# An FFN up projection by seven block products: 15 of 22 channel pairs a layer, weight sums made by accumulating transfers, W_down in four parts

## The chip, the cores and the metric

The kernel runs on one core of a Trainium2 chip in one launch. The metric is the device time in microseconds. A core has TensorE (PE, the matmuls; PEld is its loading of weights), VectorE (DVE), ScalarE (ACT), GpSimd (POOL) and SyncE (SP, which here only issues DMA). Each runs its own instructions in order and waits on semaphores for the others.

## The reference

Two layers of a decoder trunk over 512 tokens with 16 meta tokens ahead of them (L = 528), width 1024, all in float32. Each layer has a mixer (eight heads of attention with a forget gate, a convolution module, a short gated convolution, one input and one output projection) and an FFN. What matters here is the FFN:

```python
def ffn_sublayer(h, pre_g, post_g, w_up, conv_w, w_down):
    u = rms_norm(h, pre_g)
    z = jnp.einsum("bld,df->blf", u, w_up)          # 1024 -> 2 x 2816
    z = causal_depthwise_conv(z, conv_w)            # 3 taps along the tokens
    g, up = jnp.split(z, 2, axis=-1)
    y = jnp.einsum("blf,fd->bld", jax.nn.silu(g) * up, w_down)
    return h + rms_norm(y, post_g)
```

## The kernel before

Activations lie with channels on the 128 partitions and tokens along the free axis. A float32 product is made from three float32r products: every operand is split into hi (a rounded copy, by ACT) and lo (the rest, by DVE), and `mm3` issues hi by hi, lo(u) by hi(w) and hi(u) by lo(w). Half of the tokens, 264, is one matmul's width. In layer 1 the meta tokens are not needed at the end, so the halves are 250 (two tokens ahead for the taps) and 264, and in W_down one matmul of 512 takes the place of two halves in all parts but the last.

W_up has 44 tiles of 128 output channels, in 22 pairs: pair f is gate tile f and up tile 22 + f. A tile is 8 blocks of input channels x 3 x 2 halves = 48 matmuls into a pair of PSUM banks (`mmt` takes the pairs by turns). u is kept without its token factor rz; `scaled` multiplies the sums by rz while moving them from PSUM to one of four tiles z0 to z3. `ffn_gate` then makes the taps (`gate_conv`: the first tap on ACT, two on DVE), Silu on ACT, the product on DVE, and the split of the result into yhi and ylo. A group of pairs is a part (`PARTS`, 8, 7 and 7 pairs); after the pairs of a part, W_down is multiplied with them for all eight output tiles m, and the sums are copied (part 0) or added (later parts) into yp. The last part's W_down is mixed with the final norm by a planner (`finish`).

Weights stream from memory. `prep_one` loads one tile of W (512 KB, raw, three buffers, on SP's queue), and ACT and DVE split it into whi and wlo (three buffers each); `next_w` keeps two tiles ahead. Outside the planner's sections, which are `manual_schedule`, the framework's scheduler puts the instructions of each engine in order from the dependences in the code; pools of tiles with a count of buffers decide which instruction waits for which.

Of the kernel before, what the change touches and what calls it, by code (L numbers as in the profile page):

```python
# [9 lines left out]
F32 = mybir.dt.float32  # L10
# [14 lines left out]
CK = 31  # L25
DFF = 2816
NF = DFF // P
PARTS = (8, 7, 7)
AHEAD = 2
CHUNK = 1056  # L30

# [309 lines left out]
def tile_hybrid_trunk(ctx: ExitStack, tc: tile.TileContext, xT, wflat, pv_d, out):  # L341
# [89 lines left out]
    def half_sl(hf):  # L431
        return slice(H * hf, H * (hf + 1))

    def load_h(pool, src, prio=0, also=()):


        t = T(pool, [P, KD, L], F32, "h", 1)
        at = {}
        for hf in range(2):
            for k0 in range(0, KD, 2):  # L440
                eng, queue = ("act", nc.scalar) if (hf, k0) in also else ("sp", nc.sync)
                after = [at[0, KD - 2]] if also and hf else []
# [6 lines left out]
    h_dram = T(dram, [P, KD, L], F32, "h_dram")  # L449
    g_dram = [T(dram, [2, HEADS, L], F32, f"g_dram{l}") for l in range(DEPTH)]  # L450


# [23 lines left out]
    def prep_one():  # L476
        i = wpos[0]
        if i >= len(chunks):
            return
        wpos[0] += 1  # L480
# [5 lines left out]
        nc.scalar.copy(hi[:, :sz], raw[:, :sz])  # L486
        nc.vector.tensor_sub(lo[:, :sz], raw[:, :sz], hi[:, :sz].bitcast(F32))  # L487
        ready.append((i, tuple(t[:, :sz].rearrange("p (k n) -> p k n", n=n) for t in (hi, lo))))

    def prefetch(n):  # L490

        while wpos[0] < len(chunks):
            if wpos[0] not in wide and sum(i not in wide for i, _ in ready) >= n:
# [157 lines left out]
    def two(t):  # L651
        return t.rearrange("p (a b) -> p a b", a=2)
# [920 lines left out]
    def finish(norms, h, h_at, spans, ks, rhs, y_at, yp, gpost, gpre, nsplit, first=None, rz=None, scaled=None,  # L1573
# [76 lines left out]

        def ends(hf):
            a, z = spans[hf]
            yield from post_norm(norms, ("y", hf), None if first is None else ("h", hf), h, [] if merge else list(h_at.values()), a, z, yp,
                                 gpost if merge and not GA else None, None if merge else gpre, first and first.at, hf, hf, out_at, y_out)
# [70 lines left out]
    for l in range(DEPTH):  # L1725
# [20 lines left out]
        with tc.tile_pool(name=f"fp{l}", bufs=2, reuse_waits="tile") as fp:  # L1746
# [35 lines left out]
            with tc.manual_schedule(engines=every):  # L1782
# [7 lines left out]
                       gains("mix_post_g"), gains("ffn_pre_g"), SPLIT["w_out"], first, rz, scaled_half, early)  # L1790
                plan_ends()

            def wtap(i, t):
                c = _COLS["ffn_w"] + 3 * t + i
                return pv[:, c:c + 1]

            def gate_conv(t, src, dst):

                nc.scalar.activation(dst, src[:, 2:2 + 2 * fw], AF.Copy, scale=wtap(2, t))  # L1799
                for i in (1, 0):  # L1800
                    nc.vector.scalar_tensor_tensor(dst, in0=src[:, i:i + 2 * fw], scalar=wtap(i, t), in1=dst,  # L1801
                                                   op0=ALU.mult, op1=ALU.add)

            def ffn_gate(f):

                cs = []
                for e, t in enumerate((f, NF + f)):
                    c = T(fp, [P, 2, H], F32, "c", 4).rearrange("p a b -> p (a b)")[:, :2 * fw]
                    gate_conv(t, zs[(2 * f + e) % len(zs)], c)
                    cs.append(c)  # L1810
                silu = nc.scalar.activation(cs[0], cs[0], AF.Silu)  # L1811
                if f == NF - 1:
                    with tc.issue_after(silu.ins):
                        nc.scalar.preload_act_table_set(EXPSET)
                nc.vector.tensor_mul(cs[0], cs[0], cs[1])  # L1815
# [3 lines left out]
                nc.scalar.copy(ghi, cs[0])  # L1819
                nc.vector.tensor_sub(glo, cs[0], ghi.bitcast(F32))  # L1820
                return ghi, glo

            g = {}
            f0 = 0
            for part, nf in enumerate(PARTS):
                for f in range(f0, f0 + nf):
                    for i in (2 * f, 2 * f + 1):
                        if i < len(zs):
                            continue
                        if i < FIRST["w_out"]:  # L1830
                            scaled(i, [first.ps[hf, i] for hf in range(2)])
                            continue
                        w = next_w()
                        ps = mmt()
                        mm3({hf: ps[:, hf, :iws[hf]] for hf in range(2)}, w, range(KD), u_in)
                        scaled(i, [ps[:, :, :H]] if i0 == 0 else [ps[:, hf, :iws[hf]] for hf in range(2)])
                    g[f] = ffn_gate(f)
                ks = list(range(nf))
                grhs = lambda b, k, hf, f0=f0: g[f0 + k][b][:, fw * hf:fw * (hf + 1)]
                if part < len(PARTS) - 1:  # L1840
                    for m in range(KD):
                        w = next_w()
                        ps = mmt()
                        if final:

                            mm3({0: ps[:, 0, :2 * fw]}, w, ks, lambda b, k, hf, f0=f0: g[f0 + k][b][:, :2 * fw])
                            d, src = yp[:, m, t0:], ps[:, 0, :2 * fw]
                        else:
                            mm3({hf: ps[:, hf, :fw] for hf in range(2)}, w, ks, grhs)
                            d, src = two(yp[:, m, t0:]), ps[:, :, :fw]  # L1850
                        if part == 0:
                            nc.scalar.copy(d, src)  # L1852
                        else:
                            nc.vector.tensor_add(d, d, src)  # L1854
                else:
                    gpre = None if final else pvs[l + 1][1][:, _COLS["mix_pre_g"]:]
                    first = None if final else First(u_rhs, [H, H], {})
                    with tc.manual_schedule(engines=every):
# [7 lines left out]
                        finish(norms, h, {}, o_spans, ks, grhs, lambda k, nf=nf: t_last if k == nf - 1 else [], yp,  # L1866
                               gains("ffn_post_g"), gpre, SPLIT["ffn_w_down"], first)
                f0 += nf
        if final:
# [50 lines left out]
```

## Time and profile before

| | |
|---|---|
| median of 3 runs | 1326.64 us (1325.96 to 1328.13) |
| profiled execution, first to last instruction | 1324.9 us, granted TensorE clock 0.990 |
| TensorE busy | 1280.9 us, 97%, 9798 instructions |
| VectorE busy | 878.9 us, 66% |
| ScalarE busy | 643.5 us, 49% |
| GpSimd busy | 107.7 us, 8% |
| DMA moved | 118.27 MB, mean 89 GB/s |

The profiled execution has no time of its own beside its span; the span is 1.7 us under the median of the runs. A row of a view by groups gives line, engine, operation, output and inputs, shape and count, then the busy time in us and the mean of one in ns, then the idle time of the engine just ahead of them and what ended it. A row of a timeline gives start, duration, the operation, and in brackets the idle time before it and what released it. L12 is line 12 of the kernel. Most of layer 0's FFN lies between 265 and 645 us.

### The profile page before, as it was taken

The numbers are of one execution on the slowest core, as the hardware profiler recorded it, in microseconds if no ns is written. First come the engines' busy times: TensorE is split into PE (matmuls) and PEld (weight loads), VectorE is DVE, ScalarE is ACT, GpSimd is POOL, SyncE is SP. The second block draws the span as 40 slices with busy tenths as digits, with TensorE's granted clock in tenths as the row PEclk, the third lists the DMA queues.
The fourth block names the chain that finished last, engine by engine and source line by source line (L and its number), as shares of the span: only waits on it lengthen the run. The fifth ranks groups of instructions, "written<-read, shape, count | busy, mean of one in ns | idle before, by whom it ended". The sixth has DMA issues, their size and how long they took to land. (4 is left out here: it accounts for less than half of the span.)

```text
span 1324.9 us, 24035 instructions
## 1 busy us (share of the span) xinstructions
PE 1280.9 (97%) x9798; PEld 1229.1 (93%) x9798; DVE 878.9 (66%) x1516; ACT 643.5 (49%) x1221; POOL 107.7 (8%) x267
## 2 busy tenths in 40 slices
PE   6999999999999999999989999999999999999996
PEld 6988988999999999999988989889999799989995
DVE  5698887588633664566675888866877247636765
ACT  7346668655423432334661566685643233313442
POOL 1313320000000000000003233200000000000000
PEclk8999999999999999999999999999999999999998
DMA  6132120612232222323240322216032233232321
GB/s 217 49 97 60 52 93 33 209 33 87 90 96 87 89 86 90 97 93 99 95 147 17 99 76 71 57 49 221 21 96 90 86 96 94 70 113 91 90 71 64
DMA packets 42702, 118.27 MB, mean 89 GB/s; under 512 B 4848, under 2 KB 15088, under 8 KB 42592
## 3 DMA queue, kind: packets, MB, share of 16 engines
q1 hardware_dynamic: 41952, 115.94, 27.9%
q8 instruction: 77, 1.26, 0.4%
q10 hardware_dynamic: 544, 0.54, 0.1%
q14 instruction: 33, 0.27, 0.1%
q0 software_dynamic: 96, 0.26, 0.1%
HBM read 108.04 MB, written 4.33 MB: 85 GB/s over the span
## 5 line engine op out<-in xcount | busy, mean ns | idle before, releaser
L642 PE MATMUL psum<-uhi,whi 128*128 128x264 f32 (+1 forms) x1984 | 467.0, 288 | 5.2 <-ACT uhi L799 5.0
L642 PE MATMUL psum<-ulo,whi 128*128 128x264 f32 (+1 forms) x1984 | 461.1, 285 | 2.0 <-DVE ulo L800 2.0
L642 PE MATMUL psum<-uhi,wlo 128*128 128x264 f32 (+1 forms) x1984 | 459.2, 284 | 0.0
L642 PEld LDWEIGHTS psum<-uhi,whi 128*128 128x128 f32 x1984 | 332.7, 189 | 10.3 <-ACT uhi L799 5.9
L642 PEld LDWEIGHTS psum<-ulo,whi 128*128 128x128 f32 x1984 | 333.6, 189 | 3.1 <-DVE ulo L800 2.5
L642 PEld LDWEIGHTS psum<-uhi,wlo 128*128 128x128 f32 x1984 | 333.4, 189 | 0.0
L642 PE MATMUL psum<-yhi,whi 128*128 128x264 f32 (+3 forms) x840 | 235.0, 304 | 1.4 <-ACT yp L1852 1.0
L642 PE MATMUL psum<-ylo,whi 128*128 128x264 f32 (+3 forms) x840 | 232.4, 300 | 0.3 <-DVE ylo L1038 0.2
L642 PE MATMUL psum<-yhi,wlo 128*128 128x264 f32 (+3 forms) x840 | 231.7, 299 | 0.1
L486 ACT CAST whi<-raw 128x1024 fp32r<-128x1024 f32 (+1 forms) x110 | 113.4, 1032 | 212.8 <-PE psum L642 199.1
L487 DVE TENSOR_TENSOR wlo<-raw,whi 128x1024 fp32r<-128x1024 f32 (+1 forms) x110 | 131.9, 1200 | 81.6 <-ACT whi L486 79.4
L642 PEld LDWEIGHTS psum<-yhi,whi 128*128 128x128 f32 x840 | 150.0, 188 | 10.4 <-issue 1.6
L642 PEld LDWEIGHTS psum<-ylo,whi 128*128 128x128 f32 x840 | 150.0, 188 | 6.6 <-DVE ylo L1038 0.9
L642 PEld LDWEIGHTS psum<-yhi,wlo 128*128 128x128 f32 x840 | 150.1, 188 | 5.8 <-DVE wlo L611 0.5
L1801 DVE SCALAR_TENSOR_TENSOR c<-z,pv,c 128x528 f32<-128x528 f32 (+1 forms) x176 | 132.0, 756 | 2.7
L611 DVE TENSOR_TENSOR wlo<-raw,whi 128x1024 fp32r<-128x1024 f32 (+2 forms) x86 | 102.2, 1205 | 36.4 <-ACT whi L607 35.8
L607 ACT CAST whi<-raw 128x1024 fp32r<-128x1024 f32 (+2 forms) x86 | 87.6, 1034 | 33.0 <-DMA raw<-in_w_dram 16.8
L889 DVE SCALAR_TENSOR_TENSOR cacc<-apad,pv,cacc 128x528 f32<-128x528 f32 x120 | 87.6, 769 | 0.4
L1819 ACT CAST yhi<-c 128x528 fp32r<-128x528 f32 (+1 forms) x44 | 27.6, 627 | 111.3 <-DVE c L1815 111.3
L1811 ACT ACTIVATE c<-c 128x528 f32<-128x528 f32 (+1 forms) x44 | 28.1, 639 | 81.7 <-DVE c L1801 81.7
L1764 DVE TENSOR_TENSOR z<-psum,rz 128x528 f32<-128x528 f32 x40 | 28.3, 708 | 53.7 <-PE psum L642 52.2
L1799 ACT ACTIVATE c<-z,pv 128x528 f32<-128x528 f32 (+1 forms) x88 | 63.3, 726 | 0.0
(211 smaller groups left out, 1496.9 us busy)
## 6 DMA issues: line engine op xcount, KB each, us to landing
raw<-in_w_dram SPq DMA_DIRECT2D x160, 512.0 KB, 3.6
raw<-in_w_dram SPq DMA_DIRECT2D x32, 448.0 KB, 4.1
h<-in_x_dram SPq DMA_DIRECT2D x14, 264.0 KB, 5.6
raw<-in_w_dram SPq DMA_DIRECT2D x4, 528.0 KB, 4.9
q<-q SPq DMA_DIRECT2D x16, 132.0 KB, 2.6
k<-k SPq DMA_DIRECT2D x16, 132.0 KB, 2.3
h_dram<-h SPq DMA_DIRECT2D x4, 528.0 KB
h<-h_dram SPq DMA_DIRECT2D x8, 264.0 KB, 5.6
```

Of the source, the lines that this page charges most:

```text
L486: nc.scalar.copy(hi[:, :sz], raw[:, :sz])
L487: nc.vector.tensor_sub(lo[:, :sz], raw[:, :sz], hi[:, :sz].bitcast(F32))
L607: nc.scalar.copy(box["hi"][:, :sz], box["raw"][:, :sz])
L611: nc.vector.tensor_sub(lo[:, :sz], box["raw"][:, :sz], box["hi"][:, :sz].bitcast(F32))
L642: nc.tensor.matmul(d, lhsT=w[a][:, k, cols], rhs=rhs(b, k, hf), start=start and i == 0 and p == 0, stop=stop and i == n - 1 and p == 2)
L889: nc.vector.scalar_tensor_tensor(conv[j], in0=src, in1=conv[j], scalar=col("a_dw_w", CK * j + i), op0=ALU.mult, op1=ALU.add)
L1764: nc.vector.tensor_mul(two(t[:, off:]), srcs[0], two(rz))
L1799: nc.scalar.activation(dst, src[:, 2:2 + 2 * fw], AF.Copy, scale=wtap(2, t))
L1801: nc.vector.scalar_tensor_tensor(dst, in0=src[:, i:i + 2 * fw], scalar=wtap(i, t), in1=dst, op0=ALU.mult, op1=ALU.add)
L1811: silu = nc.scalar.activation(cs[0], cs[0], AF.Silu)
L1819: nc.scalar.copy(ghi, cs[0])
```

## The change

**The pairs 6 to 20 of each layer are made with seven block products.** Each pair's two weight tiles form a 2 x 2 block matrix: the gate tile's two halves over the input channels are A11 and A12, the up tile's are A21 and A22. u is cut in the same way into B11, B12, B21, B22: two halves of the input channels, two halves of the tokens (`sw`, 264 in layer 0, 258 in layer 1). One block product is 4 blocks of channels x 3 = 12 matmuls. In place of the eight products of the 2 x 2 form there are seven, with sums s1 to s4 of weight blocks and differences t1 to t4 of blocks of u: a11 by b11, a12 by b21, s4 by b22, a22 by t4, s1 by t1, s2 by t2, s3 by t3. The four outputs are sums of these, made partly in PSUM and partly as they are moved to z. Pairs 0 to 5 and pair 21 are done as before.

**The weight sums** are made by GpSimd DMAs that add to their destination (`add1` to `add3`, four a pair, 256 KB each, 120 in all), in place, in raw (three buffers) and in u (a new tile of two buffers). Each sum is then split into hi and lo as a weight (`split_s`, six buffers; `split_a22`, two).

**In part 0** `build_terms` writes h to memory (`h_mid`, loaded again after the last part), makes yp = h x g x rz, the four differences with hi and lo, and writes uhi and ulo anew from yp, so that the products need no factor afterwards. They are stored in the places of h, rs, rz and others.

**Parts are 6, 6, 5 and 5.** The last two products of a part's last pair are issued inside W_down's m = 0 (`tail`), behind the other pairs' matmuls.

```diff
-PARTS = (8, 7, 7)
+PARTS = (6, 6, 5, 5)
...
+                def load(self):
+                    self.g = T(wp, [P, CHUNK], F32, "raw", 3)
+                    self.u = T(sx, [P, 2 * self.HALF], F32, "u", 2)
+                    nc.sync.dma_start(self.g[:, :2 * self.HALF], self.src[0])
+                    nc.sync.dma_start(self.u, self.src[1])
+                    self.ga, self.gb = self.g[:, :self.HALF], self.g[:, self.HALF:2 * self.HALF]
+                    self.ua, self.ub = self.u[:, :self.HALF], self.u[:, self.HALF:]
...
+                def add1(self):
+                    nc.gpsimd.dma_start(self.ga, self.src[1][:, :self.HALF], accum_op=ALU.add)
+                    nc.gpsimd.dma_start(self.ua, self.src[1][:, self.HALF:], accum_op=ALU.add)
+
+                def add2(self):
+                    nc.gpsimd.dma_start(self.ub, self.ga, accum_op=ALU.add)
+
+                def add3(self):
+                    nc.gpsimd.dma_start(self.gb, self.ub, accum_op=ALU.add)
...
+            AHEAD_STEPS = {"load": [("load",)], "g": [("split_g",)], "add1": [("add1",)], "a22": [("split_a22",)],
+                           "add2": [("add2",)], "s31": [("split_s", "s3"), ("split_s", "s1")],
+                           "s2": [("split_s", "s2"), ("add3",)], "s4": [("split_s", "s4")]}
...
+            def p3(f):
+                d = product(banks_of(f)[0], f, "s4", "b22")
+                nc.scalar.copy(z_of(f, 0)[:, zin[1]], d[:, lap:])
+
+            def p4(f):
+                d = product(banks_of(f)[1], f, "a22", "t4")
+                z = z_of(f, 1)[:, zin[0]]
+                nc.vector.scalar_tensor_tensor(z, in0=d, scalar=-1.0, in1=z, op0=ALU.mult, op1=ALU.subtract)
+
+            def seven(f, prev, nxt, nxt2):
...
+                d = product(ba, f, "a11", "b11", True)
+                nc.scalar.copy(zg[:, zin[0]], d)
+                ahead(nxt, "g")
+                d = product(bc, f, "a12", "b21", True)
+                nc.vector.tensor_add(zg[:, zin[0]], zg[:, zin[0]], d)
+                ahead(f, "s2")
+                if prev is not None:
+                    p3(prev)
+                    conv_of(prev, 0)
+                ahead(nxt, "add1")
+                d = product(ba, f, "s2", "t2")
+                nc.scalar.copy(zu[:, zin[0]], d)
+                ahead(nxt, "a22")
+                if prev is not None:
+                    p4(prev)
+                    conv_of(prev, 1)
+                    gate_of(prev)
+                ahead(nxt2, "load")
+                d3 = product(bb, f, "s3", "t3", True)
+                ahead(nxt, "add2")
+                d = product(ba, f, "s1", "t1")
+                z = zu[:, zin[1]]
+                nc.scalar.copy(z, d[:, lap:])
+                nc.vector.scalar_tensor_tensor(z, in0=d3[:, lap:], scalar=-1.0, in1=z, op0=ALU.mult, op1=ALU.subtract)
+                ahead(f, "s4")
+                ahead(nxt, "s31")
...
+                        if m == 0 and mine:
+                            yield 0, list(range(nf - 1))
+                            tail(mine[-1])
+                            yield 1, [nf - 1]
```

**What stands where.** GpSimd, layer 0, part 1, before: the last masks of attention, the borders of z0 to z3, and then the borders of layer 1's convolution, with nothing during the FFN.

```order
L1352 AFFINE_SELECT p4w1_100_680<-p4w1_100_680 16x16
L1758 MEMSET z0_372_2908 128x2
L1758 MEMSET z1_373_2909 128x2
L1758 MEMSET z2_374_2910 128x2
L1758 MEMSET z3_375_2911 128x2
L866 MEMSET apad_743_7702 128x30
```

GpSimd now, in the same place. raw and u with the numbers 530 and 531 belong to pair 8, 548 and 549 to pair 9, 566 and 567 to pair 10, 584 and 585 to pair 11; L1957 and L1958 are add1, L1961 is add2, L1964 is add3.

```order
L1958 DMA u_549_4765<-in_w_dram 128x512
L1957 DMA raw_566_4901<-in_w_dram 128x512
L1961 DMA u_531_4628<-raw_530_4627 128x512
L1964 DMA raw_530_4627<-u_531_4628 128x512
L1958 DMA u_567_4902<-in_w_dram 128x512
L1961 DMA u_549_4765<-raw_548_4764 128x512
L1964 DMA raw_548_4764<-u_549_4765 128x512
L1957 DMA raw_584_5038<-in_w_dram 128x512
L1958 DMA u_585_5039<-in_w_dram 128x512
L1961 DMA u_567_4902<-raw_566_4901 128x512
```

The additions of a later pair (pair 10 into u_567) now stand between add3 of one pair (8) and add2 of the next (9), and the load of u_567 in turn waits until add3 of pair 8 has read u_531, whose buffer it takes.

VectorE, layer 0, at the end of the first part that has pairs by seven products (part 1) now; at the end of a part before. c is the taps' result. Before:

```order
L1764 TENSOR_TENSOR z3_375_2911<-psum_1_67,rz_371_2907 128x528
L487 TENSOR_TENSOR wlo_495_4396<-raw_493_4393,whi_494_4395 128x1024
L1801 SCALAR_TENSOR_TENSOR c_490_4383<-z3_375_2911,pv0_2_68,c_490_4383 128x528 x2
L1815 TENSOR_TENSOR c_489_4379<-c_489_4379,c_490_4383 128x528
L1820 TENSOR_TENSOR ylo7_492_4390<-c_489_4379,yhi7_491_4389 128x528
```

Now (L2003 takes the last product, a22 by t4, from PSUM; c_625 is the gate's, c_626 the up tile's):

```order
L2003 SCALAR_TENSOR_TENSOR z3_377_2913<-psum_1_67,z3_377_2913 128x264
L1811 SCALAR_TENSOR_TENSOR c_625_5389<-z2_376_2912,pv0_2_68,c_625_5389 128x528
L1942 TENSOR_TENSOR alo_661_5790<-u_655_5662,ahi_660_5789 128x512
L1811 SCALAR_TENSOR_TENSOR c_625_5389<-z2_376_2912,pv0_2_68,c_625_5389 128x528
L1811 SCALAR_TENSOR_TENSOR c_626_5407<-z3_377_2913,pv0_2_68,c_626_5407 128x528 x2
L1831 TENSOR_TENSOR c_625_5389<-c_625_5389,c_626_5407 128x528
L1836 TENSOR_TENSOR ylo5_628_5413<-c_625_5389,yhi5_627_5412 128x528
```

The gate's taps and a split of part 2's a22 now stand behind the last sum and ahead of the up tile's taps.

TensorE at the same place, now: the end of the last product a22 by t4 (h_449_3793 holds t4), then W_down of m = 0 and m = 1 (whi_609 and whi_612) for the part's fifth pair (yhi4) and its sixth and last (yhi5).

```order
L1978 MATMUL psum_1_67<-h_449_3793,alo_598_5150 128x264
L648 MATMUL psum_1_67<-yhi4_618_5306,whi_609_5216 128x264 x2
L648 MATMUL psum_1_67<-yhi4_618_5306,whi_612_5222 128x264 x2
L648 MATMUL psum_1_67<-ylo4_619_5307,whi_609_5216 128x264 x2
L648 MATMUL psum_1_67<-yhi4_618_5306,wlo_610_5217 128x264 x2
L648 MATMUL psum_1_67<-ylo4_619_5307,whi_612_5222 128x264 x2
L648 MATMUL psum_1_67<-yhi4_618_5306,wlo_613_5223 128x264 x2
L648 MATMUL psum_1_67<-yhi5_627_5412,whi_609_5216 128x264 x2
```

Twelve matmuls stand between the last product of the last pair and the first matmul on that pair's yhi. Before, all other pairs' matmuls of m = 0 and four pairs' of m = 1, 66, stood in between.

In numbers, the built program has 9229 matmuls in place of 9637; VectorE has 1723 instructions in place of 1517, ScalarE 1505 in place of 1219, GpSimd 389 in place of 269, SyncE 337 in place of 301.

More of the change, by code (lines that the diff above doesn't have):

```diff
@@ L441, in load_h @@
                 eng, queue = ("act", nc.scalar) if (hf, k0) in also else ("sp", nc.sync)
-                after = [at[0, KD - 2]] if also and hf else []
+                after = [at[0, KD - 2]] if also and hf else list(after_all)
                 at[hf, k0] = flow.op(eng, 0.5 if also else dma_us(2 * H), lambda k0=k0, hf=hf, queue=queue: queue.dma_start(
@@ L479, in prep_one @@
             return
+        assert not by_seven(i)
         wpos[0] += 1
@@ L1791, in tile_hybrid_trunk @@
                 plan_ends()
+            wxs.close()
+            sx_st = ExitStack()
+            sx = sx_st.enter_context(tc.tile_pool(name=f"sx{l}", bufs=1, side="right", reuse_waits="tile"))
             def wtap(i, t):
@@ new lines, in tile_hybrid_trunk, with unit, product @@
+            units = {}
+            def unit(f):
+                if f not in units:
+                    units[f] = Seven(f)
+                return units[f]
+            def product(bank, f, a, b, start=False):
+                d = psum[:, bank, :sw]
+                for k in range(KH):
+                    for p, (i, j) in enumerate(((0, 0), (0, 1), (1, 0))):
+                        nc.tensor.matmul(d, lhsT=unit(f).a[a][i][:, P * k:P * (k + 1)], rhs=terms[b][j][k],
+                                         start=start and k + p == 0, stop=k == KH - 1 and p == 2, skip_group_check=not start)
+                return d
@@ L1824, in tile_hybrid_trunk, with tail, skip_sevens @@
+            def tail(f):
+                p3(f)
+                conv_of(f, 0)
+                p4(f)
+                conv_of(f, 1)
+                gate_of(f)
+            def skip_sevens(n=0):
+                while wpos[0] < len(chunks) and by_seven(wpos[0]):
+                    wpos[0] += 1
+                prefetch(n)
+            build, terms_late = build_terms(), []
             f0 = 0
             for part, nf in enumerate(PARTS):
[L1826 to L1837, printed above, removed]
@@ L1838, in tile_hybrid_trunk @@
-                ks = list(range(nf))
[L1839 to L1847, printed above, removed]
-                        else:
[L1849 to L1854, printed above, removed]
-                else:
+                last = part == len(PARTS) - 1
@@ new lines, in tile_hybrid_trunk @@
+                mine = [f for f in range(f0, f0 + nf) if f in sevens]
+                coming7 = [f for f in sevens if f >= f0 + nf]
+                if part == 0:
+                    for f in range(nf):
+                        plain(f)
+                        if f:
+                            for _ in range(5):
+                                if terms_late or next(build) == "last":
+                                    terms_late.append(True)
+                                    break
+                    for _ in build:
+                        pass
```

199 lines of the change are left out of this document (183 added, 16 removed).

## The prediction

> **What bounds the kernel now.** I read the busy times first, then the busy time by stretches of the up projection, and last the rows of single groups. TensorE fills the span, and inside the up projection it is never idle at full clock:
>
> ```profile
> PE 1280.9 (97%) x9798; PEld 1229.1 (93%) x9798; DVE 878.9 (66%) x1516; ACT 643.5 (49%) x1221; POOL 107.7 (8%) x267
> 300.00:400.00 100.00, 100.00 (x822) 100.00 (x821) 62.33 (x77) 40.50 (x53) 0.00 (x0) 1.00 0.28 90
> 900.00:1000.00 100.00, 100.00 (x825) 99.57 (x824) 75.88 (x123) 54.40 (x91) 0.00 (x0) 1.00 0.31 99
> ```
>
> The last two rows are 100 us of layer 0's and of layer 1's FFN: stretch, its length, busy time (and number) of PE, PEld, DVE, ACT, POOL, then granted clock, DMA share and GB/s. A matmul costs 100/822 = 0.1217 us in layer 0 and 100/825 = 0.1212 us in layer 1, and DMA carries only 90 to 99 GB/s. So fewer matmuls shorten these stages one for one, as long as nothing else becomes late. That is what has to be found out.
>
> **What it removes.** 15 pairs a layer take 7 x 12 = 84 matmuls in place of 8 x 12 = 96. That is 180 fewer a layer: 180 x 0.1217 + 180 x 0.1212 = **-43.7 us**. The widths hardly differ (264 in place of 264; 258 in place of 264 and 250 by turns). Layer 1's last part of 5 pairs instead of 7 trades a few half-width matmuls for whole ones, under 1 us, which I leave out.
>
> **What it adds on DVE and ACT.** The rows for one operation of each kind:
>
> ```profile
> L487 DVE TENSOR_TENSOR wlo<-raw,whi 128x1024 fp32r<-128x1024 f32 x90 | 110.2, 1225 | 80.1 <-ACT whi L486 79.3
> L486 ACT CAST whi<-raw 128x1024 fp32r<-128x1024 f32 x90 | 94.6, 1051 | 167.5 <-PE psum L642 158.0 <-issue 8.6 <-ACT yp L1852 0.9
> L607 ACT CAST vlo<-raw x2: 611/614/616, 162.6 to 819.4; 128x512 fp32r<-128x512 f32 x2
> L611 DVE TENSOR_TENSOR vlo<-raw,vlo x2: 680/681/682, 163.4 to 820.3; 128x512 fp32r<-128x512 f32 x2
> L1020 DVE SCALAR_TENSOR_TENSOR rs_t<-psum,rs_t 128x264 f32<-128x264 f32 x36 | 15.2, 430 | 13.8 <-ACT rs_t L1019 13.1
> L1801 DVE SCALAR_TENSOR_TENSOR c<-z,pv,c 128x528 f32<-128x528 f32 x88 | 66.7, 765 | 1.4
> L1820 DVE TENSOR_TENSOR ylo<-c,yhi 128x528 fp32r<-128x528 f32 x22 | 15.5, 707 | 13.3 <-ACT yhi L1819 13.3
> L1799 ACT ACTIVATE c<-z,pv 128x528 f32<-128x528 f32 x44 | 32.0, 734 | 0.0
> L1819 ACT CAST yhi<-c x44: 605/626/637, 306.4 to 1274.7; 128x528 fp32r<-128x528 f32 x22, 128x512 fp32r<-128x512 f32 x22
> 299.61 5.52 DVE L1801 SCALAR_TENSOR_TENSOR c<-z,pv,c 128x528 f32<-128x528 f32 x8
> ```
>
> A pair by seven products gives DVE one split of 1024 columns (1.225), five of 512 (0.681), three sums from PSUM (0.430), four convolution taps (0.765), the product and ylo (0.707 each): 10.4 us by durations. The last row shows eight taps in 5.52 us, 0.69 each from start to start against 0.765, so back to back an operation costs about 0.08 less: 10.4 - 15 x 0.08 = 9.2 us. The pair's 84 matmuls take 84 x 0.1217 = 10.2 us. ACT has 1.05 + 5 x 0.614, two taps of 0.73, Silu and yhi of 0.63 each and three evacuations of about 0.35 (estimated as half a 528-column copy): 7.9 us. Both fit, DVE narrowly. The new waits between engines are short, like this one of PE:
>
> ```profile
> PE psum L1391 <- POOL pf L1352: 0.7, 4, 0.2
> ```
>
> I put 0.2 us on each of 30 pairs, **+6 us**, with 0 and 12 as bounds.
>
> **The ends of the parts.** Before, the last pair of a part is needed only after 66 matmuls of W_down on the other pairs, 8 us, and its chain from z to yhi took from 368.21 to 373.21:
>
> ```profile
> 368.21 0.71 DVE L1764 TENSOR_TENSOR z<-psum,rz 128x528 f32<-128x528 f32 x1 [2.26 <-PE psum L642]
> 370.24 1.57 DVE L1801 SCALAR_TENSOR_TENSOR c<-z,pv,c 128x528 f32<-128x528 f32 x2
> 371.84 0.71 DVE L1815 TENSOR_TENSOR c<-c,c 128x528 f32<-128x528 f32 x1
> 372.58 0.63 ACT L1819 CAST yhi<-c 128x528 fp32r<-128x528 f32 x1 [2.88 <-DVE c L1815]
> ```
>
> Now the last two products of the last pair are issued inside m = 0, behind the other pairs' matmuls. In the built order only 12 matmuls (1.5 us) stand between the last of a22 by t4 and the first that reads the last pair's yhi. The chain is the STT from PSUM (0.43), the gate's taps and the split of the next a22, which stand ahead on DVE (0.76 + 0.68 + 0.76, less overlaps), the two taps (1.57), the product (0.71), yhi (0.63) and about 0.3 for hops: 5.7 us. So PE waits 5.7 - 1.5 = 4.2 us at the end of parts 1 and 2 of both layers: 4 x 4.2 = **+17 us** (12 if DVE has done the gate's taps early). Before, nothing was lost there.
>
> Such a gap has a second price:
>
> ```profile
> 666.92 1.16 PE L756 MATMUL psum<-acc,om_d 128*128 128x264 f32 x4 [2.23 <-DVE acc L729]
> 717.90 0.28 PE L1140 MATMUL psum<-wlo,uhi 128*128 128x264 f32 x1
> 721.21 0.59 PE L1140 MATMUL psum<-whi,uhi 128*128 128x264 f32 x1 [3.03 <-DVE vlo L1126]
> 721.60 0.42 PE L1140 MATMUL psum<-whi,ulo 128*128 128x264 f32 x1
> 721.82 0.42 PE L1140 MATMUL psum<-wlo,uhi 128*128 128x264 f32 x1
> ...
> 724.61 0.28 PE L1140 MATMUL psum<-whi,uhi 128*128 128x264 f32 x1
> 722.00:724.00 2.00, 2.00 (x11) 2.00 (x10) 2.00 (x5) 0.00 (x0) 0.00 (x0) 0.50 0.00 0
> ```
>
> After 3.03 us of idle PE the matmuls come 0.22 apart until 724.6 at a granted clock of 0.50. From 721.21 to 724.61 it does 15 matmuls in 3.4 us, where 15 x 0.1217 = 1.8 would do: 1.6 us lost. The 2.23 us of idle ahead of 666.92 did not do that to the four matmuls right behind it, which took 1.16 us. So 4 x 1.6 = **+6.4 us**.
>
> **Part 0.** On DVE the rewriting of uhi/ulo and the making of t3 stand between the last z and the last ylo: two ulo of 1056 columns (1.26 each, from the 1.225 of 1024), one wlo of 768 (0.93), four taps (0.77), two differences, two splits, the earlier ylo, the product and ylo (0.7 each), after z itself: 11.4 us, of which yhi is there at 10.7. The cover is two m over five pairs, 60 matmuls, 7.3 us. The wait is 3.4 us, **+6.8** for two layers. That is so near the 3.03 that I leave a fall of the clock there (2 x 1.6) to the range. The Trainium skill, "TensorE: Matmul & The Clock Gate" (Part 1: The HAM clock gate), puts the idle window that throttles at about 3.4 us. The trace shows a shorter gap, of 3.03, that throttled; by the page the part ends fall and these two stay, as in my sum. The eight products that make yp (the 5.52 us above) also stand ahead of an evacuation that frees PSUM; I put 1.1 us on that, **+2.2** for both layers. h is written to memory and loaded again, hidden under W_down.
>
> **The accumulating transfers.** Each pair needs, one behind another: u's load, an addition into u's first half and g's first half, g into u's second half (add2), u's second half into g's second half (add3), and only then may the next-but-one u be loaded into that buffer, since u has two. A 256 KB accumulating transfer from GpSimd does not exist in the trace. The nearest rows:
>
> ```profile
> raw<-in_w_dram SPq DMA_DIRECT2D x160, 512.0 KB, 3.6
> q<-q SPq DMA_DIRECT2D x16, 132.0 KB, 2.6
> pv<-in_pv_dram POOLq DMA_DIRECT2D x2, 127.0 KB, 4.9
> L380 POOL DMA_DIRECT2D pv<-in_pv_dram x2: 553/638/722, 1.3 to 3.3; - x2
> 662.00:664.00 2.00, 2.00 (x15) 1.87 (x14) 1.51 (x2) 1.10 (x4) 0.00 (x0) 1.00 1.12 321
> ```
>
> Between 132 KB (2.6) and 512 KB (3.6), a plain 256 KB is 2.6 + 124/380 = 2.9 us: the lower bound X of one addition. The upper is GpSimd's own load, 4.9 for 127 KB in the crowded start, and 0.4 for the bytes to 256 KB: 5.3. An accumulating transfer must also fetch its destination, so it handles 512 KB; I take the row of 512 KB, X = **3.6**.
>
> GpSimd starts the additions in order, and the additions into u's first half for pair n+2 stand ahead of add2 of pair n+1. So the ring's cycle for a pair is u's load (3.6), that pair's addition, add2 of the pair before (issued behind it at once, landing about with it), then add3: load + 2X + 0.64 for an issue + 0.3 for hops = 3.6 + 7.2 + 0.9 = 11.7 us, against PE's 10.2. The first two units of a part are loaded during W_down before it, so the loss comes late in a part. Counted on the built order, undelayed PE wants s2 of pairs 9, 10 and 11 at 36.5, 47.2 and 58.4 us from the start of part 1, and the ring gives them at 38.5, 50.2 and 61.9: 3.5 us lost by the end. Parts 2 and 3, with five and four such pairs, lose 2.5 and 1.5. That is 7.5 a layer, **+15 us**. The traffic is 2.1 MB in 10.2 us, 206 GB/s, or 309 if the destinations count again; the last row shows 321 moved at a full share, so transfers may well be slowed by one another.
>
> The Trainium skill, "DMA: Bandwidth & Descriptors" (Anatomy of one DMA, SWDGE path), fits 2.0 us + bytes / 436,000 per us for a GpSimd transfer, an estimate of 2.6 us for 256 KB. No run here shows it for additions, and the one pair of GpSimd loads in the trace, 4.9 us for 127 KB, was slower; by the page the ring would turn in 9.7 us and cost nothing.
>
> **The sum.** The profiled execution has a span of 1324.9, and the median of the runs is 1326.6, 1.7 more, which lies around the span and which the change does not touch. 1326.6 - 43.7 + 6 + 17 + 6.4 + 6.8 + 2.2 + 15 = 1336.3: **1336 us**, 0.7% slower. By itself this case reaches from 1322 (X = 3.2, small waits 0) to 1360 (X = 4.0, where the ring costs 36).
>
> **The rivals.**
> - **The ring is free** (the other side: faster). If an addition lands within 2.9 us, the cycle is 3.6 + 5.8 + 0.9 = 10.3, level with PE. Then 1336.3 - 15 - 6 = **1315 us**, and down to 1302 if the part ends are short enough to spare the clock as well. It decides at X = 2.9, which is my lower bound; for it speaks that DMA has 70% free now and that 132 KB take 2.6, against it that the destination must be read and that the load on the queues doubles. Chance 0.36.
> - **The additions are slow.** At X = 4.5 the cycle is 13.5, 3.3 over PE, and 9 pairs a layer wait for it: 9 x 3.3 x 2 = 60 in place of 15, 1336.3 + 45 = **1381 us**, and at X = 4.8 about 1400, with gaps that cost clock. For it speaks GpSimd's row of 4.9. Chance 0.20.
> - **DVE becomes the bound**: at durations without overlap its 10.4 us, with a little waiting 10.8, 0.6 over PE in 30 pairs: +18 in place of ring and small waits, 1336.3 - 21 + 18 = **1333 us**. Against it the 0.69 of the eight taps. Chance 0.08.
> - That the products are not saved is excluded: the built program has 9229 matmuls in place of 9637, the 360 and 48 half-width ones of layer 1's last part.
>
> **How the numbers follow.** The forecast keeps 0.36. Two in ten may lie outside: below, part of the free ring's case; above, part of slow additions. From the cases I take 1302 to 1390. A measurement of this kernel can tell about 0.2%, 2.7 us, from no change. Faster: the free ring 0.36 and the forecast's low end 0.04, 0.40. The same: 0.05, from the forecast's low end and DVE's. Slower: 0.55.
>
> **What would show it.** PE should have 408 fewer matmuls, waits of 4 us for the last yhi at four part ends with a clock of 0.50 after each, about 3.4 us at the end of part 0, and waits for s2 that grow inside each part. The landing time of the additions decides: at 2.9 us I am wrong on the fast side, above 4.5 on the slow side. If the part ends show no gap, the order on DVE was not what held them.

## The result and the profile after

The changed kernel takes 1432.97 us in the median of 4 runs (1430.35 to 1436.54), the kernel before 1327.39 (1325.96 to 1328.54): a ratio of 1.080, with an interval of 1.078 to 1.082. The profiled run of it took 1430.35 us, its span is 1428.6 us. The sign and the kind of the loss were in the prediction; its size, 106 us in place of 10, was not: the range ended at 1390 us.

First the busy times, then the waits of TensorE (engine and line that waited, what for, us in total, times, longest):

```profile
PE 1289.2 (90%) x9390; PEld 1216.5 (85%) x9390; DVE 965.3 (68%) x1722; ACT 751.9 (53%) x1507; POOL 209.3 (15%) x387
```

```profile
PE psum L648 <- ACT yhi L1835: 29.4, 9, 4.4
PE psum L1978 <- ACT shi L1941: 24.6, 17, 4.3
PE psum L1978 <- ACT z L2021: 16.2, 10, 3.4
...
PE psum L1978 <- ACT z L2011: 8.1, 2, 4.6
PE psum L1978 <- ACT z L2032: 5.6, 5, 1.4
```

The 408 matmuls are gone, and TensorE is nevertheless busy for 8.3 us longer. It is idle for 1428.6 - 1289.2 = 139.4 us in place of 44.0, 95 more. The mean granted clock is 0.961 in place of 0.990, so 0.039 x 1428.6 = 56 us of clock are missing in place of 13, 42 more. That is an upper bound of the cost, since part of it falls into time in which TensorE waits anyway. 95 + 42 - 44 (the matmuls) = 93 of the 104 us by which the span grew; 10 us or a little more stand in neither row, and what they are is open.

Two groups of waits are new. The first row, for the last yhi, belongs to the ends of the parts. The others, for the split sums (shi) and for evacuations (z) that stand behind those splits in ScalarE's order, belong to the ring of adding transfers: 24.6 + 16.2 + 8.1 + 5.6 = 55 us. What the additions took, and how long a pair is:

```profile
u<-in_w_dram POOLq DMA_DIRECT2D x30, 256.0 KB, 4.0
raw<-in_w_dram POOLq DMA_DIRECT2D x30, 256.0 KB, 4.8
u<-raw POOLq DMA_DIRECT2D x30, 256.0 KB, 4.1
raw<-u POOLq DMA_DIRECT2D x30, 256.0 KB, 3.3
```

From the timelines of SyncE, GpSimd and ScalarE, layer 0, part 1, rows merged in order of time: one turn of the ring, from u's load of pair 9 (403.17) to that of pair 10 (423.07), with the load of pair 8 ahead and that of pair 13 behind. L1958 and L1957 are first additions (pair 9's u, pair 10's gate tile), L1961 and L1964 are pair 8's second and third:

```profile
384.38 0.33 SPq L1934 DMA_DIRECT2D u<-in_w_dram  x1
...
403.17 0.33 SPq L1934 DMA_DIRECT2D u<-in_w_dram  x1
407.31 0.85 POOL L1958 DMA_DIRECT2D u<-in_w_dram  x1 [5.83 <-DMA u<-in_w_dram]
409.38 1.05 ACT L1941 CAST whi<-raw 128x1024 fp32r<-128x1024 f32 x1 [4.42 <-DMA raw<-in_w_dram]
410.85 0.37 ACT L2032 COPY z<-psum 128x264 f32<-128x264 f32 x1
411.98 0.85 POOL L1957 DMA_DIRECT2D raw<-in_w_dram  x1 [3.82 <-DVE wlo L1942]
413.04 0.38 ACT L1998 COPY z<-psum 128x264 f32<-128x264 f32 x1 [1.53 <-PE psum L1978]
414.38 0.62 ACT L1941 CAST ahi<-u 128x512 fp32r<-128x512 f32 x1 [0.19 <-PE psum L1978]
416.23 0.85 POOL L1961 DMA_DIRECT2D u<-raw  x1 [3.40 <-DVE alo L1942]
419.76 0.85 POOL L1964 DMA_DIRECT2D raw<-u  x1 [2.69 <-DMA u<-raw]
423.07 0.33 SPq L1934 DMA_DIRECT2D u<-in_w_dram  x1
...
466.03 0.33 SPq L1934 DMA_DIRECT2D u<-in_w_dram  x1
```

The turn takes 19.9 us, the five from 384.38 to 466.03 take 16.3 on average, where the matmuls of a pair need 10.2 and the prediction gave the ring 11.7. It is 4.1 for u's load, then 8.9 until the second addition may start, 3.5 until that one has landed, 3.3 for the third, and then the next load. The prediction's cycle let the second addition start right behind the first; the 8.9 us were not in it. In GpSimd's order an addition for pair 10 (L1957) stands in between, and it waits 3.82 us for the split of that pair's gate tile. Then the second addition, which overwrites a22, waits 3.40 us more for a22's split. Both splits lead back to ScalarE: there the split of pair 10's gate tile (whi, 409.38) waits 4.42 us for a load, an evacuation (410.85) stands behind it, TensorE waits 1.36 us for that evacuation, the next evacuation (413.04) waits for TensorE, and only behind that comes the split of a22 (ahi, 414.38).

The part ends came as forecast in size. Layer 0: the end of part 1 with VectorE's rows ahead of it, and the end of part 3 with a row of ScalarE.

```profile
475.51 0.69 DVE L1942 TENSOR_TENSOR alo<-u,ahi 128x512 fp32r<-128x512 f32 x1
476.12 2.25 DVE L1811 SCALAR_TENSOR_TENSOR c<-z,pv,c 128x528 f32<-128x528 f32 x3
479.89 1.05 PE L648 MATMUL psum<-yhi,whi 128*128 128x264 f32 x4 [4.12 <-ACT yhi L1835]
674.81 1.28 ACT L1827 ACT_TABLE_LOAD   x1
676.79 0.39 PE L648 MATMUL psum<-yhi,whi 128*128 128x264 f32 x1 [3.72 <-ACT yhi L1835]
```

At part 1 the order is the one forecast: next a22's split and the gate's taps stand ahead of the up tile's. At part 3 it is another: yhi (676.10) stands on ScalarE behind splits of later weights, an evacuation, a Silu and a table load of 1.28 us.

### The profile page after: what moved, and what is told of

It reads as the page before. It is cut to its first block, busy times and chain, and to the rows that moved or that the text cites. A ratio compares the mean times of both kernels' runs of the same rounds, so it can differ in the third digit from the quotient of the medians.

```text
span 1428.6 us, 24192 instructions
## 1 busy us (share of the span) xinstructions
PE 1289.2 (90%) x9390; PEld 1216.5 (85%) x9390; DVE 965.3 (68%) x1722; ACT 751.9 (53%) x1507; POOL 209.3 (15%) x387
## 3 DMA queue, kind: packets, MB, share of 16 engines
q0 software_dynamic: 17376, 31.73, 13.7%
## 4 chain that ended last, share of the span: by engine, by line
PE 47%; DMA 19%; DVE 14%; issue 8%; ACT 7%; POOL 4%; POOLq 0%; DVEq 0%; SPq 0%; ACTq 0%
PE psum L648 34%; DMA raw<-u 6%; DMA raw<-in_w_dram 6%; DMA u<-raw 4%; DMA u<-in_w_dram 3%; PE psum L1978 3%; PE psum L1397 2%; DVE c L1811 2%; PE psum L1146 2%; PE psum L1340 1%; PE psum L762 1%; DVE cacc L895 1%; DVE wlo L617 1%; ACT shi L1941 1%; POOL u L1961 1%
## 5 line engine op out<-in xcount | busy, mean ns | idle before, releaser
L648 PE MATMUL psum<-uhi,whi 128*128 128x264 f32 (+1 forms) x1024 | 276.1, 293 | 12.2 <-ACT uhi L805 10.1
L648 PE MATMUL psum<-ulo,whi 128*128 128x264 f32 (+1 forms) x1024 | 269.6, 287 | 1.9 <-DVE ulo L806 1.9
L648 PE MATMUL psum<-uhi,wlo 128*128 128x264 f32 (+1 forms) x1024 | 268.8, 286 | 0.0
L648 PEld LDWEIGHTS psum<-uhi,whi 128*128 128x128 f32 x1024 | 185.6, 191 | 17.6 <-ACT uhi L805 10.9
L648 PEld LDWEIGHTS psum<-ulo,whi 128*128 128x128 f32 x1024 | 185.8, 191 | 2.9 <-DVE ulo L806 2.4
L648 PEld LDWEIGHTS psum<-uhi,wlo 128*128 128x128 f32 x1024 | 185.7, 191 | 0.0
L613 ACT CAST whi<-raw 128x1024 fp32r<-128x1024 f32 (+2 forms) x86 | 85.4, 1004 | 37.8 <-PE psum L648 21.9
L1942 DVE TENSOR_TENSOR slo<-raw,shi 128x512 fp32r<-128x512 f32 x60 | 40.8, 690 | 92.8 <-ACT shi L1941 88.2
L488 ACT CAST whi<-raw 128x768 fp32r<-128x768 f32 (+2 forms) x66 | 55.9, 846 | 87.1 <-PE psum L648 63.4
L489 DVE TENSOR_TENSOR wlo<-raw,whi 128x768 fp32r<-128x768 f32 (+2 forms) x66 | 63.9, 969 | 36.8 <-ACT whi L488 34.7
L1978 PE MATMUL psum<-h,shi 128*128 128x264 f32 (+1 forms) x240 | 53.5, 316 | 29.4 <-ACT shi L1941 21.3
```

The source lines that it names most:

```text
L613: nc.scalar.copy(box["hi"][:, :sz], box["raw"][:, :sz])
L648: nc.tensor.matmul(d, lhsT=w[a][:, k, cols], rhs=rhs(b, k, hf), start=start and i == 0 and p == 0, stop=stop and i == n - 1 and p == 2)
L1942: nc.vector.tensor_sub(lo, raw, hi.bitcast(F32))
L1978: nc.tensor.matmul(d, lhsT=unit(f).a[a][i][:, P * k:P * (k + 1)], rhs=terms[b][j][k], start=start and k + p == 0, stop=k == KH - 1 and p = ...
```

## The experiments

Each ratio is to the kernel before on the same chip, with its interval.

| run | time, us | ratio |
|---|---|---|
| changed kernel | 1433.0 | 1.080 [1.078, 1.082] |
| e1 no sums | 1342.6 | 1.012 [1.010, 1.014] |
| e2 copies for additions | 1359.1 | 1.024 [1.021, 1.026] |
| e3 three u | 1426.0 | 1.074 [1.072, 1.076] |
| e4 additions by GpSimd itself | 1365.2 | 1.029 [1.027, 1.031] |
| e5 additions in turn | 1422.2 | 1.072 [1.070, 1.073] |
| e6 no sums, last products early | 1329.1 | 1.001 [1.000, 1.002] |
| e7 before, parts 6, 6, 5, 5 | 1338.3 | 1.008 [1.007, 1.010] |
| e8 e4 and last products early | 1354.4 | 1.021 [1.018, 1.025] |
| e9 e5 and a22 loaded by itself | 1406.9 | 1.061 [1.059, 1.063] |
| e10 e5 and ScalarE's splits in turn | 1414.7 | 1.066 [1.063, 1.069] |
| e11 no sums, additions aside | 1359.3 | 1.024 [1.022, 1.026] |
| e12 before, parts 5, 5, 5, 7 | 1329.6 | 1.003 [1.002, 1.004] |
| e13 e9 with copies | 1347.4 | 1.016 [1.014, 1.018] |
| e14 e8, a22 by itself, parts 6, 5, 5, 6 | 1348.4 | 1.016 [1.015, 1.018] |

**Is it the sums at all? (e1, e2, e11)** Theory 1: the chain of adding transfers sets the pace. Theory 2: VectorE's and ScalarE's own work does.

```diff
 def add1(self):
-    nc.gpsimd.dma_start(self.ga, self.src[1][:, :self.HALF], accum_op=ALU.add)
-    nc.gpsimd.dma_start(self.ua, self.src[1][:, self.HALF:], accum_op=ALU.add)
+    pass
```

(e1; add2 and add3 alike. e2 drops `accum_op=ALU.add` in all four. e11 sends four adding transfers a pair from the weights in memory into one tile that nobody reads, started once that pair's u has landed; shi/slo have five buffers in place of six there.)

> All four adding transfers of every pair are left out, so the sums s1 to s4 are the bare weight blocks and the output is another. Theory 1 (the chain of adding transfers behind u's two buffers sets the pace, 19 us a pair in the trace after, against 10.2 us of matmuls): the waits for shi and for the evacuations behind it go, some 57 us, and with them most of the lost clock; about 1345 us, clock about 0.98, the waits for yhi at the part ends stay near 29 us. Theory 2 (VectorE's and ScalarE's own work, 10.4 and 7.9 us a pair in order, sets the pace): nothing waits for transfers but the time stays above 1400 us.

> The same transfers in the same places with the same waits, but copying instead of adding, so the sums are wrong and the bytes written are the same. If it is the adding (the destination fetched too) that makes a transfer long: landing falls from 3.3 to 4.8 us to about 3, the time to about 1390. If it is any transfer started by GpSimd, in a chain: landing and time stay, within 15 us of 1433.

> Sums left out as in e1 (the output is another), but four adding transfers of 256 KB a pair go on in step with u's loads, into a tile that nobody reads. If the traffic of the adds slows the loads enough to stall the pairs: above 1370 us. If it is only that the pairs wait for the sums: as e1, 1343 us, at most 1355.

e1 came out at 1342.6, where 1345 was expected: the sums cost 90 us, and theory 2 falls. TensorE's waits for these splits are down to 0.2 us; what leads its waits is the part ends:

```profile
PE psum L648 <- ACT yhi L1835: 21.9, 6, 4.7
```

e11 took 1359.3, a little above what was allowed for the waiting alone: the additions as mere traffic cost 17 us, which leaves 74 for waiting for the sums. And e2, with the same chain, order and bytes written, took 1359.1, where 1390 was expected: adding in place of copying is worth 74 us. The transfers of e2, by kind, and the queues' share of the 16 DMA engines, first of the changed kernel, then of e2 (packets, MB, share):

```profile
u<-in_w_dram POOLq DMA_DIRECT2D x30, 256.0 KB, 3.4
raw<-in_w_dram POOLq DMA_DIRECT2D x30, 256.0 KB, 3.1
u<-raw POOLq DMA_DIRECT2D x30, 256.0 KB, 2.8
raw<-u POOLq DMA_DIRECT2D x30, 256.0 KB, 2.3
```

```profile
q0 software_dynamic: 17376, 31.73, 13.7%
```

```profile
q0 software_dynamic: 9696, 31.73, 6.8%
```

A copy lands in 2.3 to 3.4 us, an addition in 3.3 to 4.8. For the same 31.73 MB the additions take twice the engines' time and 1.8 times the packets: the destination does count. A copy lands about where the prediction's lower bound stood (2.9), three of the four kinds of addition above the 3.6 that it took.

**Which links hold the ring? (e3, e5, e9, e10, e13)**

```diff
-self.u = T(sx, [P, 2 * self.HALF], F32, "u", 2)
+self.u = T(sx, [P, 2 * self.HALF], F32, "u", 3)
```

(e3; shi/slo five buffers in place of six, here and in e9, e13 and e14. What the sixth is worth was not tried by itself.)

> u has three buffers (and shi/slo five in place of six, to make room). Theory 1: u's load of the next-but-one pair no longer waits for the add of the pair before, so 4 us of u's load leave the cycle: about 1385 us. If GpSimd's order (the adds of a later pair ahead of the second add of the earlier) is the chain, and not the buffers: within 15 us of 1433.

Only 7 us less. The loads of u run one pair further ahead, but the third additions of pairs 7 and 8 stand at 400.67 and 420.11, where they were at 399.75 and 419.76. So u's two buffers, the reason that the prediction gave for the ring, are not what holds it.

```diff
 def add1(self):
-    nc.gpsimd.dma_start(self.ga, ...)
-    nc.gpsimd.dma_start(self.ua, ...)
+    with tc.issue_after(last3[0].ins) if last3 else nullcontext():
+        nc.gpsimd.dma_start(self.ga, ...)
+        nc.gpsimd.dma_start(self.ua, ...)
```

(e5: a pair's first additions come behind the pair before's last one on GpSimd.)

> Only GpSimd's order is changed: the additions of a pair start after the last one of the pair before, so nothing of a later pair stands ahead of an earlier pair's second addition. Theory 1a (the head of GpSimd's queue, waiting for a later pair's load and split, makes the 19 us cycle): two buffers of u then allow a pair in 2 x 4.1 + 1.7 = 10 us, level with the matmuls; about 1375 us. Theory 1b (the landing time of each link alone, whatever the order): within 15 us of 1433.

11 us less, not 58. Theory 1a, that GpSimd's order is the loop, falls as the main cause. Its wait moved to the next link in line (GpSimd's waits in e5; L1962 is the second addition):

```profile
POOL u L1962 <- DVE alo L1942: 142.8, 17, 15.1
```

This is the split of a22 again. e9 takes it out of the ring by loading A22 a second time, e10 only changes ScalarE's order:

```diff
+self.v = T(sx, [P, self.HALF], F32, "v", 2)
+nc.sync.dma_start(self.v, self.src[1][:, self.HALF:])
...
-self.split(("a22",), self.ub, sx, ("ahi", "alo"), 2, self.HALF)
+self.split(("a22",), self.v, sx, ("ahi", "alo"), 2, self.HALF)
```

```diff
-nc.scalar.copy(hi, raw)
+with tc.issue_after(last_a22[0].ins) if last_a22 and names[0] == "a11" else nullcontext():
+    x = nc.scalar.copy(hi, raw)
```

> As e5, and a22 is split from a load of its own (256 KB more a pair, tile v; shi/slo five buffers), so that u's second half waits for no split before the second addition. In e5 the second addition waited for alo up to 15 us behind ScalarE's queue. Theory 1c (the loop closes through the split of a22, which stands in order behind splits that wait for a later pair's transfers): the waits of L1961 for alo go and some 40 us with them, about 1380 us. If the landing times alone make the loop: within 15 us of e5's 1422.

> As e5, and on ScalarE the split of a later pair's gate tile may only be issued after the split of a22 of the pair before; no transfer and no operation more or less. Theory 1c: the same 40 us, or half of it, as other splits still stand in the way: 1380 to 1400 us. Landing times alone: within 10 us of 1422.

e9 is 15 us below e5 and e10 8 us: the link is real, but less than half of the 40 expected of it. In e9, past the first two pairs of each part (which wait for their gate tile's split), GpSimd's additions wait for nothing but landings. L1964 is the second, L1967 the third:

```profile
POOL raw L1967 <- DMA u<-raw: 133.4, 29, 7.3
POOL u L1964 <- DMA raw<-in_w_dram: 127.1, 30, 6.4
```

So either the landings are the loop now, or other parts of the order are. e13 is e9 with copies:

> As e9, with copying in place of adding transfers (the sums are wrong, the output is another); the order and all waits are e9's. In e9 a pair takes about 13.4 us from one load of u to the next, all of it links of transfers: u's load, one addition, the second, the third. If the landing time of adding transfers under this traffic is what is left of the loop: a cycle of 10 to 11 us and 1345 to 1360 us. If something else in the order of the engines holds it: above 1385 us.

1347.4 us, 59 less than e9, near the lower end of what landings alone would give. The loads of u in the timelines of SyncE, of e9 and of e13:

```profile
401.15 0.33 SPq L1934 DMA_DIRECT2D u<-in_w_dram  x1
...
455.10 0.33 SPq L1934 DMA_DIRECT2D u<-in_w_dram  x1
```

```profile
396.36 0.33 SPq L1934 DMA_DIRECT2D u<-in_w_dram  x1
...
438.28 0.33 SPq L1934 DMA_DIRECT2D u<-in_w_dram  x1
```

Four turns in 54.0 us, 13.5 each, with additions, and four in 41.9, 10.5 each, with copies: about the 10.2 of the matmuls. The two landings for which GpSimd waits in each turn, first in e9, then in e13:

```profile
raw<-in_w_dram POOLq DMA_DIRECT2D x30, 256.0 KB, 5.6
u<-raw POOLq DMA_DIRECT2D x30, 256.0 KB, 4.8
```

```profile
raw<-in_w_dram POOLq DMA_DIRECT2D x30, 256.0 KB, 3.6
u<-raw POOLq DMA_DIRECT2D x30, 256.0 KB, 3.9
```

By these medians they take 10.4 us together as additions and 7.5 as copies, 2.9 less for a turn that is 3.0 shorter. With copies the matmuls may already hold the turn, so 3.0 is the least that the additions cost it. So the ring's cause is shown. Each turn holds landings in a row, and an adding one takes longer than a copy: 0.6 to 1.7 us by kind between the changed kernel and e2, 0.9 to 2.8 between e9 and e13. What stands in order on GpSimd and ScalarE adds waits to it: 26 us from the changed kernel to e9, and 12 with copies, from e2 to e13.

**The part ends and the parts (e6, e7, e12)**

```diff
 if m == 0 and mine:
-    yield 0, list(range(nf - 1))
     tail(mine[-1])
-    yield 1, [nf - 1]
-else:
-    yield 0, list(range(nf))
+yield 0, list(range(nf))
...
+with tc.issue_after(last_mm[0].ins) if part and m < 2 else nullcontext():
     mm3(...)
```

(e6 and e8: the last two products are in the program ahead of W_down's m = 0 and 1.)

> As e1 (sums left out, so the output is another), and the last pair's last two products are issued before W_down's m = 0 and 1 of parts 1 and 2 instead of behind most of them, so that 60 matmuls cover the chain to the last yhi. If the part ends are what is left of the loss in e1: four waits of 3.7 to 4.7 us and the half clock after them go, 4 x (4.0 + 2.5) = 26 us: about 1317 us, with the waits at part 0 and part 3 left. If VectorE is behind by then anyway: above 1335.

The waits for yhi at the ends of parts 1 and 2 are gone (21.9 in 6 before, 5.3 in 2 now, both of part 3), but the time fell by 13.5 us and not by 26. W_down had also filled the waits of the last pairs' products, and without it 5 us of these came back, as I read it (TensorE's timeline of e6, the largest of them):

```profile
538.70 0.39 PE L1978 MATMUL psum<-yhi,shi 128*128 128x264 f32 x1 [2.36 <-ACT z L2021]
```

TensorE's idle time fell by 10 us (1340.8 - 1259.4 = 81.4 in e1, 1327.8 - 1256.1 = 71.7 in e6), the missing clock by 6 (a mean of 0.973 and 0.977), where 16 and 10 were expected. What sets off the half clock that stayed was not tried one by one.

> The kernel before with parts of 6, 6, 5 and 5 and nothing else of the change. The part ends' stalls should come from the late last two products, not from the parts: 1325 to 1330 us. If shorter parts by themselves leave too little cover: 1340 us or more.

> The kernel before with parts of 5, 5, 5 and 7. e7 (6, 6, 5, 5) cost 11.5 us, most of it a wait of 5.9 us for uhi and half clock where layer 0 ends. If that comes from the short last part, whose W_down has less to put under the final norm: 1327 to 1331 us. If it comes from having four parts: about 1338.

e7 refuted the expectation: parts of 6, 6, 5 and 5 alone cost 11.5 us. e12, also four parts, but 7 in the last, costs 2.7. So it is the short last part. In e7's timeline of TensorE at the end of layer 0, where the kernel before waited 2.23 us for acc, 1.09 for uhi and 0.46 for ulo:

```profile
669.57 2.05 PE L756 MATMUL psum<-acc,om_d 128*128 128x264 f32 x8 [2.65 <-DVE acc L729]
673.73 1.16 PE L756 MATMUL psum<-c,om_d 128*128 128x264 f32 x4 [1.22 <-ACT c L720]
680.81 0.59 PE L642 MATMUL psum<-uhi,whi 128*128 128x264 f32 x1 [5.93 <-ACT uhi L799]
```

That the last part's W_down is what is laid under the final norm's steps there is argued from this, not shown.

**Without transfers (e4, e8, e14)**

```diff
-nc.gpsimd.dma_start(self.ub, self.ga, accum_op=ALU.add)
+nc.gpsimd.tensor_add(self.ub, self.ub, self.ga)
```

> The four sums are made by GpSimd's own additions in SBUF (128x512, in place) instead of adding transfers, so nothing is left out of the computation. Theory 1: an addition of some 1 us in place of a transfer of 4 us, and no wait for a landing: about 1345 us as without sums. Rival: GpSimd's additions are slow (over 2 us) or slow VectorE's rows down: above 1380 us.

> As e4 (sums by GpSimd's own additions) with the products of e6 ahead of W_down; nothing is left out of the computation. 26 us less than e4 if the two causes add: about 1339 us; if GpSimd's chain is late at the part ends, above 1350.

> Nothing left out: the sums by GpSimd's own additions, the last products ahead of W_down as in e8, a22 from a load of its own as in e9, and parts of 6, 5, 5 and 6, so that the last part is longer. In e4 the second addition waited 74 us for alo, which goes; about 15 us from that and 6 us from the last part off e8's 1354: 1333 us. If GpSimd's additions slow VectorE, so that it sets the pace: above 1345 us.

e4 saves 68 of the 90 us and ends at 1365, where 1345 was expected. e8 saves another 11 (its runs reach from 1351.7 to 1362.1), e14 6 more: 1354 and 1348, where 1339 and 1333 were expected, and none beats the kernel before. What is left between e4 and e1, 23 us, I read as VectorE's, which no run tries by itself: its split of the gate tile in e1 and in e4, and GpSimd's own additions in e4 (groups by line; busy time, mean ns):

```profile
L1942 DVE TENSOR_TENSOR wlo<-raw,whi 128x1024 fp32r<-128x1024 f32 x30 | 36.6, 1224 | 32.2 <-ACT whi L1941 31.3
```

```profile
L1942 DVE TENSOR_TENSOR wlo<-raw,whi 128x1024 fp32r<-128x1024 f32 x30 | 48.9, 1631 | 33.8 <-ACT whi L1941 33.3
```

```profile
L1964 POOL TENSOR_TENSOR raw<-raw,u 128x512 f32<-128x512 f32 x30 | 52.0, 1733 | 2.4
```

GpSimd adds 512 columns in 1.5 to 1.7 us, and VectorE's split beside it takes a third longer on average. The Trainium skill, "SBUF — State Buffer" (SBUF: two separate sides), says that GpSimd and a VectorE operation with two SBUF inputs exclude one another on a shared pair of ports; the two VectorE rows agree with it, 1.224 us and 1.631.

## Why the prediction was wrong

- **The accumulating transfers** were the step that failed: +15 us in the sum, 90 by e1. The cycle of 11.7 us for a turn of the ring (load + 2X + issue + hops) was wrong; the five turns from 384.38 to 466.03 took 16.3 us on average. Three parts of it failed.
  - The price X of one addition was 3.6 by the row of 512 KB; by kind it was 3.3 to 4.8, about 4.05 on average. The argument that the destination counts was right (13.7% against 6.8%), but not enough for a transfer that meets others on the way. By itself this is the smaller part: at X = 4.0 the prediction's own cycle puts the ring at 36 us and the time at 1360.
  - The cycle went through u's two buffers. A third one saved 7 us (e3).
  - The cycle left out what stands in order. a22's split, for which the second addition waits, was on the same tile and could have been read from the code. And only GpSimd was looked at as an engine in order, not ScalarE, whose splits wait for landings and hold up the evacuations behind them: that is how a late transfer reached TensorE as "z" (30 us of waits). Nor did the waits grow inside a part, as was forecast: the largest of layer 0's part 1, 4.58 us, ended at 397.40, early in it.
- **The rival of slow additions** came nearest, 1381 us at X = 4.5 and about 1400 at 4.8, but on the same cycle. Only one kind of addition took more than 4.5 us; it was the cycle that was longer.
- **The gain** was right as a count: 408 fewer matmuls. It shows in e6, which has the changed kernel's parts and no sums: against before TensorE idles 28 us more and 17 us more of clock are missing, which just about uses up the 43.7. Of that loss e7 gives 11.5 to the parts.
- **The clock** was under-counted: 6.4 us in the sum, up to 42 measured. e1, without the additions, has 23 of these, so the ring brought only the other 20. The six waits of 2.9 us or more in the ring were all followed by half clock, two of them (the waits of 4.58 and 3.54 us) for twice as long as the 3.4 us in the trace of before. The waits of 3.25 and 3.20 us at part 0 were followed by it too (0.50 from 357.5 to 360.5 and from 1061 to 1067), which the prediction left to its range. And the trace of before has a clock of 0.50 from 669.9 to 673.3 as well, right after the waits of 2.23 and 1.09 us; the prediction looked only at the four matmuls between them.
- **The part ends** were right: waits of 4.2 us each were forecast for parts 1 and 2, and 4.1, 3.7, 3.0 and 4.4 came; 3.4 was forecast for part 0, and 3.25 and 3.2 came. The two ends of part 3, 3.7 and 3.8, were missed.
- **The shorter last part** was not priced at all, 11.5 us by e7.
- **The small waits** and VectorE as the bound (10.4 us of work in 10.2) did not show as a loss: in e1, with VectorE at the same work, TensorE waits 0.5 us in all for splits and evacuations of the pairs. Some 7 us of e1's waits, for the differences (tiles acc, rs and rz) where part 1 begins, were not foreseen.
- The row of GpSimd's own load, 4.9 us, was nearer to most of the additions' 3.3 to 4.8 than the 2.6 estimated from the Trainium skill's "DMA: Bandwidth & Descriptors" (Anatomy of one DMA, SWDGE path), by which the ring would have cost nothing; a copy took 2.3 to 3.4.

## What to carry to other kernels

A chain of transfers that feeds a loop turns no faster than every wait of one turn added up, so write the turn down as a chain through the code, with each reader that must be done before the next write, and each engine on which a link stands in order behind something else that waits. A further buffer helps only where the buffer is the link that waits; here it bought 7 us of 90. An addition in a transfer is not a copy: here it took a fifth to a half longer to land and twice the DMA time. And when filler work is moved to the front, ask which later wait it was covering; here W_down covered either the pairs' products or the part's end, not both.

## What the runs showed of the hardware

An adding transfer of 256 KB lands in 3.3 to 4.8 us where a copy takes 2.3 to 3.4 (changed kernel and e2; 3.4 to 6.3 and 2.5 to 3.9 in e9 and e13), costs GpSimd 0.85 us to start in place of 0.54, and takes the DMA engines twice the time for its bytes (13.7% and 6.8% of the span for 31.73 MB):

```profile
L1961 POOL DMA_DIRECT2D u<-raw x30: 841/852/1192, 376.4 to 1352.3; - x30
```

```profile
L1961 POOL DMA_DIRECT2D u<-raw x30: 536/536/538, 378.7 to 1286.1; - x30
```

(The tile u of the changed kernel and of e2: start of the second addition, min/median/max ns.) And one gap can cost more than one stretch at half clock. Windows of e1 around the end of part 3, layer 0 (stretch, length, PE, PEld, DVE, ACT and POOL busy, clock): a wait of 3.71 us ends at 635.5, and the clock is at half from 634 to 640.

```profile
634.00:637.00 3.00, 1.37 (x4) 1.07 (x5) 1.51 (x3) 2.77 (x4) 0.00 (x0) 0.50 0.83 283
637.00:640.00 3.00, 3.00 (x16) 3.00 (x15) 2.08 (x3) 0.63 (x1) 0.00 (x0) 0.50 0.03 9
640.00:643.00 3.00, 3.00 (x24) 3.00 (x24) 0.00 (x0) 0.00 (x0) 0.00 (x0) 0.88 0.00 0
```
